# Score maps worked in pairs, and the sparse heads' normalising given to Pool

## The chip, the cores and the metric

The kernel runs on one core of one Trainium2 chip. A core has five engines that matter here: TensorE (PE, with its weight loads as PEld), VectorE (DVE), ScalarE (ACT), GpSimd (Pool, POOL in the rows) and SyncE (SP, which issues the transfers). The metric is the device time of one execution in microseconds (us). The time of the kernel before is a median of 760.54 us over 3 runs (760.04 to 768.84).

## The reference, cut to what matters

The program is a decoder trunk of two layers on 256 tokens of width 1024, in float32. Each layer is an attention part and a SwiGLU part, both with RMSNorm before, and a shift, a scale and a gate that come from a conditioning vector `c` (`ada_w`, six 1024-wide products a layer).

```python
h = rms_norm(x, attn_norm[i]) * (1.0 + sc_a) + sh_a
y = sparse_mixer(h, ...)  if i % 2 == 0 else  diff_mixer(h, ...)
x = x + g_a * y
h = rms_norm(x, ffn_norm[i]) * (1.0 + sc_f) + sh_f
x = x + g_f * swiglu(h, w_gate, w_up, w_down)
...
p = masked_softmax(q @ k.T * scale, causal)      # one map: 256 queries x 256 keys, 64 deep
o_nsa = g0 * o_c + g1 * (p_s @ v_s) + g2 * (p_w @ v_w)    # layer 0, 8 NSA heads, two full maps each
o_moba = p @ v                                   # layer 0, 8 MoBA heads, one map each
a = p[:, :, 0] - lam * p[:, :, 1];  o = a @ v    # layer 1, 8 differential heads, two maps each
```

With 256 tokens every block that the sparse heads could choose is taken, so their maps are plain causal ones. That makes 16 NSA maps, 8 MoBA maps and 16 differential maps: 40 in all. The 24 maps of layer 0 are divided by their row sums (for NSA also multiplied by a gate) before they meet the values; in layer 1 the division comes after the product.

## The kernel before, in words

A weight product is made from two-part numbers: `split` (L181 to L184) writes a high part with ACT (L182) and the rest with DVE (L183), and three products are added. Nearly every matmul goes through the helper `mm`, so L110 stands for all of them; they are told apart by the names of their tiles.

One softmax map is `softmax_map` (L799 to L813). Its causal 256x256 matrix lies in one PSUM bank as two parts: the first 128 queries against 128 keys (128 columns) and the other 128 queries against 256 keys (256 columns). PE makes both (four instructions, since a float32 matmul passes twice); for each part DVE masks, scales and finds the row extreme (L808), and ACT takes the exponential with its row sum (L810). `normalise` (L816) then multiplies by the factor: part 0 on ACT (L819), part 1 on DVE (L821). `transpose_map` (L824) turns the three 128x128 blocks on PE (L827) into another bank, and ACT copies them to SBUF (`pT`, L829). `av` (L832) multiplies with the values.

Queries and keys of a head take 64 of the 128 rows of PE, and its output 64 of the 128 columns: the even head of a pair stands on rows and columns 0 to 63, the odd one on 64 to 127. In `nsa_heads` (L1061) a pair `pr` runs over its two heads, a head over its two branches (`kTn`, `nkv` are the keys and values), and after both branches come `av` twice and a product for the compressed branch (`pcT` by `vblk`). `moba_heads` (L1100, keys and queries `kTm`, `qTm`, values `vm`) has one map for a head. `diff_heads` (L1134) makes two maps for a head and combines them; it has no `normalise`.

The order on each engine is set by a scheduler that simulates the program with its own costs; the Python generators hand it the work, and a `yield` is where `weave` (L40) may go over to another generator, by the shares written beside each. In layer 0 the heads are woven with `moba_proj` and `ada` at first, and then with `ada_pe` (L310): 16 steps, each a 512 KB transfer and a product on four groups of 32 columns of PE (`raw`, `cs` in the rows), that fill PE between the maps. After them comes the output projection with `sp_w_out`. The buffers: four `s` tiles (one a map), three `pT` tiles, five `raw` tiles; banks for scores `SC`, for transposes `TR` and for outputs `OT`.

Of the kernel before, what the change touches and what calls it, by code (L numbers as in the profile page):

```python
# [13 lines left out]
AF = mybir.ActivationFunctionType  # L14
ALU = mybir.AluOpType
AX = mybir.AxisListType

P = 128
S = 256
# [39 lines left out]
def tile_trunk(ctx: ExitStack, tc: tile.TileContext, x, c, positions, ada_w, ada_b, attn_norm, ffn_norm,  # L59
# [36 lines left out]
    def tmp(shape, tag, bufs, dt=F32):  # L96
        return sp.tile(shape, dt, name=nm(tag), tag=tag, bufs=bufs)
# [10 lines left out]
    def mm(o, lhsT, rhs, start, stop):  # L108

        ins = T.matmul(o, lhsT=lhsT, rhs=rhs, start=start, stop=stop).ins  # L110
        key = o.tensor.name
        if start and key in closed:
            tc.add_manual_dep(ins, closed[key], mybir.DependencyInfo(mybir.DependencyClass.NoSync,
                                                                    mybir.DependencyReason.DATA))
        if stop:
            closed[key] = ins.name
        if chain:
            if chain[0]:
                tc.add_manual_dep(ins, chain[0], mybir.DependencyInfo(mybir.DependencyClass.NoSync,
                                                                     mybir.DependencyReason.DATA))  # L120
            chain[0] = ins.name
        return ins
# [673 lines left out]
        return fcol[:, n:n + 1]  # L796


    def softmax_map(qh, kh, nr):  # L799

        b = bank(*SC)
        mm(b[:, 0:P], lhsT=qh[:, 0:P], rhs=kh[:, 0:P], start=True, stop=True)
        mm(b[:, P:P + S], lhsT=qh[:, P:S], rhs=kh, start=True, stop=True)
        s = tmp([P, 384], "s", 4)
        mx = tmp([P, 2], "mx", 6)
        sm = tmp([P, 2], "sm", 6)
        for t, (o, n) in enumerate(((0, P), (P, S))):
            V.tensor_tensor_reduce(out=s[:, o:o + n], in0=b[:, o:o + n], in1=maskc[:, S - n:S], scale=nr(t),  # L808
                                   scalar=3e38, op0=ALU.add, op1=ALU.min, accum_out=mx[:, t:t + 1])
            A.activation(out=s[:, o:o + n], in_=s[:, o:o + n], func=AF.Exp, scale=-1.0, bias=mx[:, t:t + 1],  # L810
                         accum_out=sm[:, t:t + 1])
        return s, sm

    SEG = ((0, P), (P, S))

    def normalise(s, sm):  # L816
        for t, (o, n) in enumerate(SEG):
            if t == 0:
                A.activation(out=s[:, o:o + n], in_=s[:, o:o + n], func=AF.Copy, scale=sm[:, t:t + 1])  # L819
            else:  # L820
                V.tensor_scalar(out=s[:, o:o + n], in0=s[:, o:o + n], scalar1=sm[:, t:t + 1], scalar2=None,  # L821
                                op0=ALU.mult)

    def transpose_map(s):  # L824
# [12 lines left out]

    def nsa_first(hts):
# [222 lines left out]
    def nsa_heads(oh, ol):  # L1061
        qT, nrs, kT, vv, gts, vblk, pcT = (box[k] for k in ("qT", "nrs", "kT", "vv", "gts", "vblk", "pcT"))
        for pr in range(4):
            g = pr // 2
            ob = None
            for half in range(2):
                h = pr * 2 + half
                rows = slice(half * 64, (half + 1) * 64)
                pTs = []
                for br in range(2):  # L1070
                    s, sm = softmax_map(qT[rows, pr, :], kT[rows, br, g, :], lambda t: nrs[:, t, h:h + 1])
                    V.reciprocal(out=sm, in_=sm)
                    V.tensor_tensor(out=sm, in0=sm, in1=gts[:, :, (1 + br) * 8 + h], op=ALU.mult)
                    normalise(s, sm)
                    pTs.append(transpose_map(s))
                    yield
                if ob is None:
                    ob = bank(*OT)
                o = ob[rows, 0:S]
                for br in range(2):  # L1080
                    av(o, lambda kc: vv[kc][:, 1 + br, g, :], pTs[br], br == 0, False)
                mm(o, lhsT=vblk[:, h, :], rhs=pcT, start=False, stop=True)
            anc.append(split(ob[:, 0:S], oh[:, pr, :], ol[:, pr, :])[::-1])
            yield

# [14 lines left out]
    def moba_heads(oh, ol):  # L1100
        qT, kT, v, nrs = (box2[k] for k in ("qT", "kT", "v", "nrs"))
        for pr in range(4):
            ob = None
            for half in range(2):
                h = pr * 2 + half
                rows = slice(half * 64, (half + 1) * 64)
                s, sm = softmax_map(qT[rows, pr, :], kT[rows, pr, :], lambda t: nrs[:, t, h:h + 1])
                V.reciprocal(out=sm, in_=sm)
                normalise(s, sm)
                pT = transpose_map(s)  # L1110
                if ob is None:
                    ob = bank(*OT)
                av(ob[rows, 0:S], lambda kc: v[kc][:, h * 64:(h + 1) * 64], pT, True, True)
                yield
            anc.append(split(ob[:, 0:S], oh[:, pr, :], ol[:, pr, :])[::-1])
            yield

# [16 lines left out]
    def diff_heads(part, st, oh, ol):  # L1134
# [15 lines left out]
        for pr in range(2):  # L1150
            od = tmp([P, 512], "od", 2).rearrange("p (h t d) -> p h t d", h=2, t=NT)
            ss = tmp([P, 4], "dss", 3)
            for h2 in range(2):
                hh = pr * 2 + h2
                ps = []
                for cmp_ in range(2):
                    rows = slice(cmp_ * 64, (cmp_ + 1) * 64)
                    ps.append(softmax_map(qT[rows, hh, :], kT[rows, hh, :],
                                          lambda t: nrs[:, t, hh * 2 + cmp_:hh * 2 + cmp_ + 1]))
                    yield  # L1160

                (s0, m0), (s1, m1) = ps
                V.reciprocal(out=m1, in_=m1)
# [32 lines left out]
    def late(*gens):  # L1196
        for g in gens:
            yield from g
# [71 lines left out]
```

## Time and profile before

| what | value |
|---|---|
| median of 3 runs | 760.54 us (760.04 to 768.84) |
| the profiled execution | 761.66 us, its span 760.0 us |
| mean granted TensorE clock | 0.973 |
| NSA and MoBA maps of layer 0 | about 82 to 202 us of the span |
| differential maps, part 0 with the projection of part 1 | about 470 to 530 us |
| PE, DVE, ACT, POOL busy over the span | 720.1, 499.3, 397.6, 49.3 us |

The profile is of one execution, and its own time is 1.1 us above the median. A busy share is a mean over the span; the rows further down are read from one stretch each, as time and length of a group of instructions.

### The profile page before, as it was taken

How to read it: one execution, taken by the hardware profiler on the slowest of the kernel's cores; microseconds unless marked ns; L12 is line 12 of the kernel's file. 1: busy time of each engine (PE TensorE's matmuls, PEld its weight loads, DVE VectorE, ACT ScalarE, POOL GpSimd, SP SyncE). 2: the span in 40 equal slices, each digit the busy share in tenths (PEclk: the TensorE clock that was granted, in tenths of full speed). 3: DMA queues.
4: the chain of work that ended last, by engine and by line, in shares of the span. 5: the costliest groups of instructions: out<-in, count | busy, mean ns of one | idle time of the engine just before them, and what ended most of it. 6: DMA issues, size and time to landing. Idle time of an engine off the chain costs nothing.

```text
span 760.0 us, 11877 instructions
## 1 busy us (share of the span) xinstructions
PE 720.1 (95%) x4414; PEld 586.9 (77%) x4414; DVE 499.3 (66%) x1032; ACT 397.6 (52%) x755; POOL 49.3 (6%) x131
## 2 busy tenths in 40 slices
PE   5889999999989999999999799979899999999997
PEld 1468567555679989999898578767679999999985
DVE  3558567654588788877776685787587584544532
ACT  3465635666666555345363566866466344434430
POOL 5004102000000000000000023230000000000000
PEclk9999899999999999999999999997889999999999
DMA  9965188126847999999995366152145886566501
GB/s 320 379 234 192 38 305 280 45 106 218 279 147 239 340 324 324 346 318 329 314 321 191 111 209 206 63 190 81 47 135 190 269 293 202 168 195 191 173 25 55
DMA packets 90625, 159.47 MB, mean 210 GB/s; under 512 B 6199, under 2 KB 56508, under 8 KB 90568
## 3 DMA queue, kind: packets, MB, share of 16 engines
q1 hardware_dynamic: 90088, 158.72, 62.1%
q8 instruction: 34, 0.56, 0.3%
q14 instruction: 23, 0.19, 0.1%
q0 software_dynamic: 480, 0.01, 0.0%
HBM read 157.66 MB, written 1.05 MB: 209 GB/s over the span
## 4 chain that ended last, share of the span: by engine, by line
PE 86%; ACT 4%; DVE 4%; DMA 3%; issue 2%; POOL 1%; SPq 0%; ACTq 0%; DVEq 0%
PE bank L110 82%; PE bank L827 2%; ACT s L810 1%; DMA vm<-in_ada_w_dram 1%; DMA tok<-in_ada_w_dram 1%; DVE lo L183 1%; ACT hi L182 1%; DMA raw<-in_sp_w_in_dram 1%; PE bank L632 1%; ACT bigT L182 1%; PE bank L393 1%; DVE w2k L402 0%; DVE bigT L183 0%; DVE s L1167 0%; DVE xs L428 0%
## 5 line engine op out<-in xcount | busy, mean ns | idle before, releaser
L183 DVE TENSOR_TENSOR lo<-raw,hi 128x1024 fp32r<-128x1024 f32 x144 | 172.3, 1208 | 88.5 <-ACT hi L182 87.9
L182 ACT ACTIVATE hi<-raw 128x1024 fp32r<-128x1024 f32 x144 | 149.2, 1047 | 132.7 <-PE bank L110 72.2
L110 PE MATMUL bank<-hi,bigT 128*128 128x512 f32 (+2 forms) x640 | 195.2, 382 | 15.0 <-ACT bigT L182 13.5
L110 PEld LDWEIGHTS bank<-hi,bigT 128*128 128x128 f32 x640 | 119.7, 198 | 41.8 <-ACT bigT L182 16.0
L110 PE MATMUL bank<-bigT,hi 128*128 128x256 f32 x768 | 140.0, 283 | 0.0
L110 PEld LDWEIGHTS bank<-bigT,hi 128*128 128x128 f32 x768 | 120.3, 191 | 1.7 <-issue 0.9
L110 PE MATMUL bank<-lo,bigT 128*128 128x512 f32 (+2 forms) x320 | 119.5, 374 | 0.0
L110 PE MATMUL bank<-bigT,lo 128*128 128x256 f32 x384 | 108.6, 283 | 0.0
L271 DVE SCALAR_TENSOR_TENSOR ada_acc<-araw,cs,ada_acc 128x1024 f32<-128x1024 f32 x60 | 76.8, 1280 | 30.3 <-DMA araw<-in_ada_w_dram 29.9
L110 PEld LDWEIGHTS bank<-bigT,lo 128*128 128x128 f32 x384 | 73.6, 192 | 0.0
L110 PEld LDWEIGHTS bank<-lo,bigT 128*128 128x128 f32 x320 | 63.2, 198 | 10.3 <-issue 1.4
L808 DVE CUSTOM_DVE_ANT_0 s<-bank,maskc,nrs 128x128 f32<-128x128 f32 x80 | 29.8, 414 | 31.4 <-PE bank L827 21.4
L810 ACT ACTIVATE s<-s,mx 128x128 f32<-128x128 f32 x80 | 35.6, 448 | 8.1 <-DVE mx L808 8.1
L152 POOL TENSOR_SCALAR rs_w<-ss 128x16 f32<-128x16 f32 x7 | 4.8, 684 | 430.7 <-DVE ss L610 388.7
L183 DVE TENSOR_TENSOR nkv<-raw,nkv 128x1024 fp32r<-128x1024 f32 x16 | 19.6, 1222 | 12.9 <-ACT nkv L182 12.9
L110 PE MATMUL bank<-hi,kTm 128*128 128x512 f32 x80 | 27.6, 402 | 0.0
L110 PE MATMUL bank<-hi,vm 128*128 128x512 f32 x80 | 27.5, 400 | 0.0
L182 ACT ACTIVATE nkv<-raw 128x1024 fp32r<-128x1024 f32 x16 | 16.9, 1055 | 20.1 <-PE bank L110 9.8
L183 DVE TENSOR_TENSOR tok<-raw,tok 128x1024 fp32r<-128x1024 f32 x18 | 22.0, 1221 | 5.7 <-ACT tok L182 5.5
L110 PE MATMUL bank<-bigT,nkv 128*128 128x256 f32 x192 | 25.7, 281 | 0.0
L427 DVE TENSOR_TENSOR xn<-bank,mod 128x512 f32<-128x512 f32 x16 | 11.0, 690 | 20.9 <-PE bank L110 20.9
L110 PE MATMUL bank<-bigT,tok 128*128 128x256 f32 x192 | 24.7, 277 | 0.0
(322 smaller groups left out, 1174.8 us busy)
## 6 DMA issues: line engine op xcount, KB each, us to landing
araw<-in_ada_w_dram SPq DMA_DIRECT2D x66, 512.0 KB, 5.0
raw<-in_ffn_w_gate_dram SPq DMA_DIRECT2D x44, 512.0 KB, 5.5
raw<-in_ffn_w_up_dram SPq DMA_DIRECT2D x44, 512.0 KB, 5.2
raw<-in_ffn_w_down_dram SPq DMA_DIRECT2D x44, 512.0 KB, 4.7
raw<-in_diff_w_in_dram SPq DMA_DIRECT2D x24, 512.0 KB, 5.1
raw<-in_sp_w_in_dram SPq DMA_DIRECT2D x20, 512.0 KB, 6.2
raw<-in_ada_w_dram SPq DMA_DIRECT2D x17, 512.0 KB, 4.8
raw<-in_nsa_cmp_w_dram SPq DMA_DIRECT2D x8, 512.0 KB, 4.7
```

Of the source, the lines that this page charges most:

```text
L110: ins = T.matmul(o, lhsT=lhsT, rhs=rhs, start=start, stop=stop).ins
L152: E.tensor_scalar(out=o, in0=i, scalar1=m, scalar2=c_, op0=ALU.mult, op1=ALU.add)
L182: i1 = A.activation(out=hi, in_=src, func=AF.Copy)
L183: i2 = V.tensor_tensor(out=lo, in0=src, in1=hi.bitcast(F32), op=ALU.subtract)
L271: ins = V.scalar_tensor_tensor(out=acc, in0=raw, scalar=cs[:, k:k + 1], in1=acc, op0=ALU.mult, op1=ALU.add)
L393: T.transpose(out=(b[k % 2] if type(b) is tuple else b)[:, k * P:(k + 1) * P], in_=xn[:, f * 512 + k * P:f * 512 + (k + 1) * P], identity= ...
L427: V.tensor_tensor(out=y, in0=bs[t][f], in1=g[:, fs], op=ALU.mult)
L632: T.transpose(out=b[:, k * P:(k + 1) * P], in_=src[:, k * P:(k + 1) * P], identity=ident)
L808: V.tensor_tensor_reduce(out=s[:, o:o + n], in0=b[:, o:o + n], in1=maskc[:, S - n:S], scale=nr(t), scalar=3e38, op0=ALU.add, op1=ALU.min, ...
L810: A.activation(out=s[:, o:o + n], in_=s[:, o:o + n], func=AF.Exp, scale=-1.0, bias=mx[:, t:t + 1], accum_out=sm[:, t:t + 1])
L827: T.transpose(out=b[:, k * P:(k + 1) * P], in_=s[:, k * P:(k + 1) * P], identity=ident)
```

## The change

Two heads' maps (for a differential head its two maps) are worked together. `softmax_maps` makes the first part of both scores, then the second part of both, and goes part by part through DVE and ACT. `av` takes the outputs, values and `pT` tiles of both heads and alternates between them. Pool multiplies both parts of a layer 0 map by the factors, in place of ACT and DVE. In `nsa_heads` the loop over branches is now inside the pair, a pair of maps ends with one `yield`, and `av` stands behind it. The `pT` tiles are four, the row extremes have a tile for each part, `first` takes 6 yields of the NSA heads into the first weave instead of 10, and the differential heads' share is 12 instead of 16.

```diff
-    def softmax_map(qh, kh, nr):
+    def softmax_maps(qks, nrs):
+        bs = [bank(*SC) for _ in qks]
+        for n in range(2):
+            for b, (qh, kh) in zip(bs, qks):
+                if n == 0:
+                    mm(b[:, 0:P], lhsT=qh[:, 0:P], rhs=kh[:, 0:P], start=True, stop=True)
+                else:
+                    mm(b[:, P:P + S], lhsT=qh[:, P:S], rhs=kh, start=True, stop=True)
+        res = [(tmp([P, 384], "s", 4), tmp([P, 2], "sm", 6)) for _ in qks]
         for t, (o, n) in enumerate(((0, P), (P, S))):
+            for b, nr, (s, sm) in zip(bs, nrs, res):
+                mx = tmp([P, 2], "mx", 6)
...
     def normalise(s, sm):
         for t, (o, n) in enumerate(SEG):
-            if t == 0:
-                A.activation(out=s[:, o:o + n], in_=s[:, o:o + n], func=AF.Copy, scale=sm[:, t:t + 1])
-            else:
-                V.tensor_scalar(out=s[:, o:o + n], in0=s[:, o:o + n], scalar1=sm[:, t:t + 1], scalar2=None,
-                                op0=ALU.mult)
+            G.tensor_scalar(out=s[:, o:o + n], in0=s[:, o:o + n], scalar1=sm[:, t:t + 1], scalar2=None, op0=ALU.mult)
...
-        pT = tmp([P, 384], "pT", 3)
+        pT = tmp([P, 384], "pT", 4)
...
-    def av(o, v, pT, first, last):
-        mm(o, lhsT=v(0), rhs=pT[:, 0:S], start=first, stop=False)
-        mm(o[:, P:S], lhsT=v(1), rhs=pT[:, S:S + P], start=False, stop=last)
+    def av(os, vs, pTs, first, last):
+        for o, v, pT in zip(os, vs, pTs):
+            mm(o, lhsT=v(0), rhs=pT[:, 0:S], start=first, stop=False)
+        for o, v, pT in zip(os, vs, pTs):
+            mm(o[:, P:S], lhsT=v(1), rhs=pT[:, S:S + P], start=False, stop=last)
...
+            for br in range(2):
+                res = softmax_maps([(qT[e * 64:(e + 1) * 64, pr, :], kT[e * 64:(e + 1) * 64, br, g, :])
+                                    for e in range(2)],
+                                   [lambda t, h=pr * 2 + e: nrs[:, t, h:h + 1] for e in range(2)])
                 pTs = []
+                for e, (s, sm) in enumerate(res):
                     V.reciprocal(out=sm, in_=sm)
...
                     normalise(s, sm)
                     pTs.append(transpose_map(s))
+                yield
+                av(os, [lambda kc: vv[kc][:, 1 + br, g, :]] * 2, pTs, br == 0, False)
+            for e, o in enumerate(os):
+                mm(o, lhsT=vblk[:, pr * 2 + e, :], rhs=pcT, start=False, stop=True)
...
-    weave((late(np_, first(nh, 10)), 22), (moba_proj(hts), 20), (ada(0, 2, pin=True), 9))
+    weave((late(np_, first(nh, 6)), 22), (moba_proj(hts), 20), (ada(0, 2, pin=True), 9))
...
-    weave((diff_heads(0, st, *oa), 16), (diff_proj(hts, 1, st), 18))
+    weave((diff_heads(0, st, *oa), 12), (diff_proj(hts, 1, st), 18))
```

The scheduler orders the engines anew. On PE in the heads of layer 0, before: `ident,s` are transposes of a map, `raw,cs` passes of `ada_pe`, `kTm,qTm` scores, `pT,nkv` the product with the values (256 columns, then 128), `pcT,vblk` the compressed branch.

```order
L827 MATMUL bank_71<-ident,s_1668 128x128 x3
L110 MATMUL bank_70<-raw_1704,cs 1x256 x4
L110 MATMUL bank_68<-kTm_787,qTm_786 128x128
L110 MATMUL bank_68<-kTm_787,qTm_786 128x256
L110 MATMUL bank_73<-pT_1645,nkv_110 64x256
L110 MATMUL bank_73<-pT_1645,nkv_111 64x128
L110 MATMUL bank_73<-pcT_1140,vblk_843 64x256
L827 MATMUL bank_72<-ident,s_1687 128x128 x3
L110 MATMUL bank_69<-kTm_787,qTm_786 128x128
L110 MATMUL bank_69<-kTm_787,qTm_786 128x256
```

And the same place in the changed kernel:

```order
L110 MATMUL bank_73<-pT_1639,nkv_110 64x256
L828 MATMUL bank_71<-ident,s_1668 128x128
L110 MATMUL bank_70<-raw_1888,cs 1x256 x4
L828 MATMUL bank_71<-ident,s_1668 128x128 x2
L110 MATMUL bank_73<-pT_1648,nkv_110 64x256
L110 MATMUL bank_73<-pT_1639,nkv_111 64x128
L110 MATMUL bank_73<-pT_1648,nkv_111 64x128
L110 MATMUL bank_73<-pcT_1140,vblk_843 64x256 x2
L828 MATMUL bank_72<-ident,s_1670 128x128
L110 MATMUL bank_68<-kTm_787,qTm_786 128x128
L110 MATMUL bank_68<-kTm_787,qTm_786 128x256
L828 MATMUL bank_72<-ident,s_1670 128x128 x2
```

The two heads' `pT,nkv` products stand together except for the first one's 256 columns, the two `pcT,vblk` products stand together, and some maps' three transposes are cut into one and two with other work between. Scores are still ordered one map after the other in this piece.

On POOL in layer 0, of the changed kernel: `rs_a`, `rs_y` are steps of the inverse root that scales the MoBA keys, twelve small operations in a row before; L823 is the new multiplication.

```order
L155 TENSOR_TENSOR rs_a_931<-rs_a_931,rs_w_929 128x16
L823 TENSOR_SCALAR s_1161<-s_1161,sm_1162 128x128
L823 TENSOR_SCALAR s_1161<-s_1161,sm_1162 128x256
L823 TENSOR_SCALAR s_1238<-s_1238,sm_1239 128x128
L823 TENSOR_SCALAR s_1238<-s_1238,sm_1239 128x256
L823 TENSOR_SCALAR s_1240<-s_1240,sm_1241 128x128
L823 TENSOR_SCALAR s_1240<-s_1240,sm_1241 128x256
L161 TENSOR_SCALAR rs_a_931<-rs_a_931 128x16
```

Six of the new operations stand between two steps of that chain, and two more a step ahead of them.

On PE in layer 1, at the end of the projection of part 1, before: the last two of 24 weight products (`hi`, `lo` by `bigT`), and then the transposes of keys and queries (L632, `tok`), of a head's output (L1145) and of a map.

```order
L110 MATMUL bank_67<-lo_5057,bigT_2134 128x512
L110 MATMUL bank_67<-hi_5056,bigT_2135 128x512
L632 MATMUL bank_73<-ident,tok_4688 128x128 x4
L632 MATMUL bank_74<-ident,tok_4893 128x128 x4
L1145 MATMUL bank_70<-ident,od_4586 128x128 x2
L632 MATMUL bank_73<-ident,tok_4893 128x128 x4
L827 MATMUL bank_73<-ident,s_4947 128x128 x3
L110 MATMUL bank_68<-kTm_4564,qTm_4563 128x128
```

In the changed kernel the 24 weight products begin behind those transposes (their first two are shown):

```order
L632 MATMUL bank_74<-ident,tok_4725 128x128 x4
L632 MATMUL bank_73<-ident,tok_4725 128x128 x4
L828 MATMUL bank_74<-ident,s_4796 128x128 x3
L632 MATMUL bank_73<-ident,tok_4929 128x128 x4
L110 MATMUL bank_70<-vm_4270,pT_4838 128x128 x3
L632 MATMUL bank_74<-ident,tok_4929 128x128 x4
L828 MATMUL bank_73<-ident,s_4979 128x128 x3
L110 MATMUL bank_69<-kTm_4588,qTm_4587 128x128
L1145 MATMUL bank_70<-ident,od_4610 128x128 x2
L110 MATMUL bank_67<-hi_4996,bigT_2156 128x512
L110 MATMUL bank_67<-lo_4997,bigT_2156 128x512
```

What moved: the transposes that needed the keys and queries now have the weight products behind them instead of ahead of them.

## Rows read from the trace of the kernel before

**Rows 1.** Page: busy us (share of the span) and instructions; chain by engine.

```profile
PE 720.1 (95%) x4414; PEld 586.9 (77%) x4414; DVE 499.3 (66%) x1032; ACT 397.6 (52%) x755; POOL 49.3 (6%) x131
...
PE 86%; ACT 4%; DVE 4%; DMA 3%; issue 2%; POOL 1%; SPq 0%; ACTq 0%; DVEq 0%
```

**Rows 2.** Windows of 60 us: PE, PEld, DVE, ACT, POOL busy, clock, DMA share, GB/s.

```profile
140.00:200.00 60.00, 58.73 (x378) 31.54 (x376) 30.02 (x133) 40.98 (x129) 0.00 (x0) 1.00 0.42 145
```

**Rows 3.** Timeline, PE, 140 to 200 us: start, length, line, tiles, PE rows*columns, shape.

```profile
152.50 0.55 PE L827 MATMUL bank<-ident,s 128*128 128x128 f32 x3
152.98 0.92 PE L110 MATMUL bank<-kTn,qT 64*128 64x128 f32 x4
153.83 0.86 PE L110 MATMUL bank<-pT,nkv 128*64 128x256 f32 x4
154.62 0.87 PE L827 MATMUL bank<-ident,s 128*128 128x128 f32 x6
155.43 0.92 PE L110 MATMUL bank<-kTn,qT 64*128 64x128 f32 x4
156.28 0.86 PE L110 MATMUL bank<-pT,nkv 128*64 128x256 f32 x4
156.98 0.59 PE L110 MATMUL bank<-pcT,vblk 128*64 128x256 f32 x2
157.50 0.92 PE L110 MATMUL bank<-kTn,qT 64*128 64x128 f32 x4
...
174.96 0.59 PE L110 MATMUL bank<-raw,cs 128*1 128x256 f32 x2
...
177.29 0.61 PE L110 MATMUL bank<-raw,cs 128*1 128x256 f32 x8
...
180.39 0.93 PE L110 MATMUL bank<-kTm,qTm 64*128 64x128 f32 x8
```

**Rows 4.** Groups by line and shape, ACT, then DVE, 140 to 200 us.

```profile
L810 ACT ACTIVATE s<-s,mx 128x256 f32<-128x256 f32 x18 | 9.0, 501 | 0.0
L819 ACT ACTIVATE s<-s,sm 128x128 f32<-128x128 f32 x18 | 6.9, 394 | 1.0 <-DVE sm L1073 0.8 <-DVE sm L1108 0.2
...
L183 DVE TENSOR_TENSOR lo<-raw,hi 128x1024 fp32r<-128x1024 f32 x4 | 4.8, 1224 | 3.8 <-ACT hi L182 3.8
```

**Rows 5.** Groups by line and shape, POOL, whole span.

```profile
L766 POOL TENSOR_SCALAR_AFFINE_SELECT maskc<-maskc 128x256 f32<-128x256 f32 x1 | 0.5, 467 | 0.0
...
L130 POOL TENSOR_SCALAR_AFFINE_SELECT ident<-ones 128x128 f32<-128x128 f32 x1 | 0.3, 284 | 0.0
```

**Rows 6.** Timelines, POOL and DVE, around 63 and 89 us.

```profile
63.49 1.16 POOL L152 TENSOR_SCALAR rs_y<-rs_w 128x16 int32<-128x16 int32 x1
...
63.37 1.23 DVE L183 TENSOR_TENSOR lo<-raw,hi 128x1024 fp32r<-128x1024 f32 x1
...
88.85 0.20 POOL L152 TENSOR_SCALAR rs_y<-rs_w 128x16 int32<-128x16 int32 x1
```

**Rows 7.** Timeline, PE, around 510 us; in brackets the idle time before.

```profile
509.36 0.66 PE L632 MATMUL bank<-ident,tok 128*128 128x128 f32 x4 [2.44 <-ACT kTm L633]
511.55 0.90 PE L827 MATMUL bank<-ident,s 128*128 128x128 f32 x3 [1.53 <-ACT qTm L633]
```

**Rows 8.** Windows of 5 us around there, columns as in rows 2.

```profile
510.00:515.00 5.00, 3.46 (x16) 2.54 (x15) 3.68 (x9) 2.41 (x7) 0.00 (x0) 0.50 0.83 261
515.00:520.00 5.00, 5.00 (x21) 3.61 (x21) 4.66 (x24) 4.07 (x19) 0.00 (x0) 0.50 0.63 209
520.00:525.00 5.00, 5.00 (x24) 3.70 (x24) 3.59 (x18) 3.44 (x16) 0.00 (x0) 0.63 0.00 0
```

**Rows 9.** Chains of waits around 95 us and 500 us: start, length, what.

```profile
94.30 5.79 DMA raw<-in_sp_w_in_dram
...
500.34 5.48 PE bank L110 x24
...
514.57 2.27 ACT s L810 x10
```

More of the change, by code (lines that the diff above doesn't have):

```diff
@@ L796, in fc @@
         return fcol[:, n:n + 1]
-    def softmax_map(qh, kh, nr):
[L801 to L806, printed above, removed]
-        for t, (o, n) in enumerate(((0, P), (P, S))):
[L808 to L812, printed above, removed]
+    def softmax_maps(qks, nrs):
[7 more added lines that the diff above has]
+        res = [(tmp([P, 384], "s", 4), tmp([P, 2], "sm", 6)) for _ in qks]
+        for t, (o, n) in enumerate(((0, P), (P, S))):
+            for b, nr, (s, sm) in zip(bs, nrs, res):
+                mx = tmp([P, 2], "mx", 6)
+                V.tensor_tensor_reduce(out=s[:, o:o + n], in0=b[:, o:o + n], in1=maskc[:, S - n:S], scale=nr(t),
+                                       scalar=3e38, op0=ALU.add, op1=ALU.min, accum_out=mx[:, t:t + 1])
+                A.activation(out=s[:, o:o + n], in_=s[:, o:o + n], func=AF.Exp, scale=-1.0, bias=mx[:, t:t + 1],
+                             accum_out=sm[:, t:t + 1])
+        return res
     SEG = ((0, P), (P, S))
@@ L1064, in nsa_heads @@
             g = pr // 2
[L1065 to L1068, printed above, removed]
+            ob = bank(*OT)
+            os = [ob[e * 64:(e + 1) * 64, 0:S] for e in range(2)]
+            for br in range(2):
+                res = softmax_maps([(qT[e * 64:(e + 1) * 64, pr, :], kT[e * 64:(e + 1) * 64, br, g, :])
+                                    for e in range(2)],
+                                   [lambda t, h=pr * 2 + e: nrs[:, t, h:h + 1] for e in range(2)])
                 pTs = []
-                for br in range(2):
-                    s, sm = softmax_map(qT[rows, pr, :], kT[rows, br, g, :], lambda t: nrs[:, t, h:h + 1])
+                for e, (s, sm) in enumerate(res):
                     V.reciprocal(out=sm, in_=sm)
-                    V.tensor_tensor(out=sm, in0=sm, in1=gts[:, :, (1 + br) * 8 + h], op=ALU.mult)
+                    V.tensor_tensor(out=sm, in0=sm, in1=gts[:, :, (1 + br) * 8 + pr * 2 + e], op=ALU.mult)
                     normalise(s, sm)
                     pTs.append(transpose_map(s))
[L1076 to L1082, printed above, removed]
+                yield
+                av(os, [lambda kc: vv[kc][:, 1 + br, g, :]] * 2, pTs, br == 0, False)
+            for e, o in enumerate(os):
+                mm(o, lhsT=vblk[:, pr * 2 + e, :], rhs=pcT, start=False, stop=True)
             anc.append(split(ob[:, 0:S], oh[:, pr, :], ol[:, pr, :])[::-1])
@@ L1102, in moba_heads @@
         for pr in range(4):
[L1103 to L1107, printed above, removed]
+            res = softmax_maps([(qT[e * 64:(e + 1) * 64, pr, :], kT[e * 64:(e + 1) * 64, pr, :]) for e in range(2)],
+                               [lambda t, h=pr * 2 + e: nrs[:, t, h:h + 1] for e in range(2)])
+            pTs = []
+            for s, sm in res:
                 V.reciprocal(out=sm, in_=sm)
                 normalise(s, sm)
[L1110 to L1114, printed above, removed]
+                pTs.append(transpose_map(s))
+            yield
+            ob = bank(*OT)
+            av([ob[e * 64:(e + 1) * 64, 0:S] for e in range(2)],
+               [lambda kc, h=pr * 2 + e: v[kc][:, h * 64:(h + 1) * 64] for e in range(2)], pTs, True, True)
             anc.append(split(ob[:, 0:S], oh[:, pr, :], ol[:, pr, :])[::-1])
@@ L1154, in diff_heads @@
                 hh = pr * 2 + h2
[L1155 to L1160, printed above, removed]
+                ps = softmax_maps([(qT[e * 64:(e + 1) * 64, hh, :], kT[e * 64:(e + 1) * 64, hh, :]) for e in range(2)],
+                                  [lambda t, h=hh * 2 + e: nrs[:, t, h:h + 1] for e in range(2)])
+                yield
                 (s0, m0), (s1, m1) = ps
```

## The prediction, as it was made
> **What bounds the kernel now.** I read the page first, for the engine that sets the pace: PE is busy 95% of the span and 86% of the chain that ended last runs over it, while POOL has 6% [rows 1]. Then the stretch that the change touches most, layer 0's heads: from 140 to 200 us PE is busy 58.73 of 60 us at the full clock, ACT 40.98, DVE 30.02, POOL not at all [rows 2]. So taking work from ACT and DVE buys next to nothing by itself; what counts is how long PE's own instructions take there, and the timeline of PE prices them one by one [rows 3]. Last, layer 1's heads, where PE is not full: it stands idle 2.44 and 1.53 us for ACT's copies of keys and queries [rows 7], and its clock is at the lower of its two levels, 1.2 instead of 2.4 GHz, for 5 + 5 + (1 - 0.63) x 2 x 5 = 13.7 us [rows 8].
>
> **Prices of PE's pieces**, from one start to the next in [rows 3]: three transposes of a map 152.98 - 152.50 = 0.48; six 155.43 - 154.62 = 0.81, so three more cost 0.33 and a group of its own 0.15; scores of one map 153.83 - 152.98 = 0.85; its product with the values (AV) 154.62 - 153.83 = 0.79; the compressed branch (PC) 157.50 - 156.98 = 0.52. Two maps' scores that stand side by side, eight instructions on both halves of PE's rows, last 0.93 against 0.92 for four: the second map is free. The same holds for groups of columns, shown by the passes of `ada_pe`: eight on four groups last 0.61, two on one group 0.59.
>
> **The change on PE, layer 0.** The work is the same; what is saved is counted in the new order.
> - Scores: of 24 maps seven pairs stand side by side and ten maps alone, so 17 times 0.85 are paid; before there were about 21. Saved: 4 x 0.85 = 3.4.
> - AV: twelve pairs. In one all four steps are adjacent, which saves one map's 0.79. In eleven the first head's 256 columns stand alone (0.15 + 2/3 of 0.64 = 0.58) and the other three steps follow together (0.43 + 0.21 + 0.15 = 0.79): 1.37 against 1.58 saves 0.21. Together 11 x 0.21 + 0.79 = 3.1.
> - PC: eight become four pairs: 4 x 0.52 = 2.1.
> - Transposes: twelve maps' three transposes are cut in two, others are joined; groups go from 23 to 32: 9 x 0.15 = 1.35 lost. This row is a price that PE pays at each change of the tile shape. The Trainium skill, "TensorEngine Tiling (Array Packing)", Key Properties, says that a change of tiling mode drains the engine, which speaks against cutting these groups; it gives no figure, and its other property, that tiles work independently, is what the eight-instruction row shows.
>
> Sum 3.4 + 3.1 + 2.1 - 1.35 = 7.3, taken as 7. Bounds: if nothing on different columns overlaps, as it does for `ada_pe` but is not shown for AV, AV and PC give nothing and 3.4 - 1.35 = 2 is left. If every pair overlapped fully, scores would save 9 x 0.85, AV 12 x 0.79, PC 2.1: 19. I stay near the count, since it is made of rows at each term.
>
> **POOL's new work.** 24 maps times two operations. No row shows a 128x256 multiply there; the nearest are its 128x128 and 128x256 selects, 0.284 and 0.467 [rows 5], which I take: 0.75 a map, 1.5 a pair, about 1.8 with gaps. From below the 0.20 of a small one; from above 1.16, what the same small one took while DVE ran `lo<-raw,hi`, 1.23 long, from 63.37 [rows 6]. PE needs per pair of NSA maps 2 x (0.85 + 0.48 + 0.79) + 0.52 = 4.76 before and, less 7.3 / 12, about 4.15 after. So POOL at 1.8 hides behind PE. Its factors come later than now: ACT and DVE did the two parts at once in 0.394 [rows 4], and the second map of a pair now waits 1.5, some 1.1 longer; four `s` tiles let the other pair's 4.15 of PE work stand in between, so I cost that at nothing. If that cover were gone it would be 12 x 1.1 = 13. ACT and DVE lose one operation each per map, off the path, costed at nothing. On POOL's queue the eight multiplications within the chain of the MoBA keys make it end some 3 us later (four maps at 0.75); the projection's next weights land 5.79 after 94.30 [rows 9], and PE has other work until then, so again nothing; uncovered it would be 3. The transfers keep their order; `ada_pe` ends earlier among the heads and the output weights move in between, off the path. The fourth `pT` and the separate extremes take a wait away at most, nothing.
>
> **Layer 1.** The scores of a head's two maps stood side by side already, so pairing gains nothing there. What moves is the 24 weight products, 5.48 us [rows 9], from ahead of the transposes to behind them, with ACT's copies ahead of four splits. At best both idle times go, 3.97, and of the half clock about 2, since the chain after it runs over ACT's exponentials, 2.27 [rows 9], and not over PE alone: 6. At worst the products then wait for their own splits and nothing is won: 0. I take 1.5, about one of the two idle times, for the products still have to be done before the heads of part 1 and the exponentials set the pace behind them.
>
> **Sum.** -7 - 1.5 = -8.5 on the profiled execution's 761.66 gives 753.2; that execution stands 1.1 above the median of the runs, so **752** is the predicted time. A measurement of this kernel can tell about 2%, 15 us, from no change.
>
> **Rivals.**
> - *Layer 1 opens up.* Idle times and lower clock both go: 4.5 more, 747; with the pairs of layer 0 at somewhat better than the count, 743. For: ACT's copies, which released both waits [rows 7], now stand ahead of the splits. Against: the exponentials behind. Chance 0.14.
> - *POOL becomes the pace* (slower). Each multiplication shares its time with a DVE operation of two SBUF inputs and takes 1.2 as in [rows 6]; four and gaps make 5.1 a pair, more than PE's 4.76 before: 12 x 0.35 = +4, and PE's holes may bring its clock to the lower level, at most another 6.8 for a stretch as long as the 13.7 in [rows 8]: 765 to 771. It decides from (4.15 - 0.3) / 4 = 0.96 an operation; beyond +2% it is at 4.76 + 15.2 / 12 = 6.0 a pair, 1.4 an operation. Against: from 140 to 200 us there are only four such DVE operations of 1.22 [rows 4]; the first pairs and the last MoBA pairs meet more. Chance 0.12, a third of it beyond 2%. The Trainium skill, "SBUF — State Buffer", Who interferes with whom, has this as a rule: a DVE instruction with two SBUF inputs holds the shared read port against a GpSimd one that reads SBUF, and the later one waits in full. The two lengths of the small operation agree with it, 1.16 beside such an instruction and 0.20 without.
> - *Pairing doesn't do what it says.* The instructions stand close but the first of each pair waits for the second head's `pT` or bank, and the saved time comes back as waits (most of the 7): 757 to 762. For: PE takes its instructions in order, and both heads' exponentials now come before one AV. Chance 0.19.
> - *Full overlap in layer 0*, all 19: 740. Against: the counted order. Chance 0.03.
>
> My forecast, 747 to 757, has the remaining 0.52. The range 743 to 766 leaves out the last case and the part of the second beyond it. Faster by over 2%, below 745.3: 0.03 and half of the first, 0.10. Slower, above 775.7: 0.04. Within 2%: 0.86.
>
> **What would show it.** Right: in the heads of layer 0 PE stays busy, the count of AV and PC groups falls, adjacent AV steps of two heads last about 0.8, the new multiplications last near 0.3 and 0.45, and the output projection starts some 7 us earlier. Layer 1: the idle time before L632 shrinks. Wrong: multiplications of 1 us and more, PE waiting for POOL ahead of transposes, a clock below 1.00 between 90 and 200 us, or AV pairs that last 1.6 in spite of standing together.

## The result, and the profile after

The changed kernel takes 766.72 us (median of 20 runs, 762.45 to 774.45), the kernel before 761.13 us beside it (median of 20). The ratio is **1.0072, interval 1.0049 to 1.0094**: slower by some 5.5 us, where I had forecast 752 us in a range of 743 to 766. The profiled execution of the changed kernel took 762.45 us, 4.3 below its median, and its span is 760.7 us: it lies with the fastest executions, so one loss below had to be read from the experiments' profiles too.

The page, busy times and chain, against [rows 1]:

```profile
PE 712.7 (94%) x4414; PEld 577.5 (76%) x4414; DVE 492.3 (65%) x1008; ACT 392.2 (52%) x731; POOL 87.4 (11%) x179
...
PE 81%; ACT 5%; DVE 4%; issue 4%; DMA 4%; POOL 1%; SPq 1%; POOLq 0%; ACTq 0%; DVEq 0%
```

PE is busy 7.4 us less than before, and the span is no shorter: what PE saves comes back as idle time. In the heads of layer 0 this is seen in a window of 60 us as in [rows 2], then in the slowest ten, then in what follows (length; PE, PEld, DVE, ACT, POOL busy; clock):

```profile
140.00:200.00 60.00, 58.12 (x373) 31.08 (x372) 29.27 (x117) 38.22 (x113) 29.90 (x36) 0.91 0.57 191
142.00:152.00 10.00, 9.18 (x42) 5.93 (x42) 4.66 (x19) 5.12 (x19) 3.85 (x4) 0.52 0.00 1
160.00:208.00 48.00, 48.00 (x322) 25.41 (x315) 23.73 (x79) 29.74 (x80) 21.76 (x26) 1.00 0.81 271
```

From 142 to 152 us the clock is 0.52, nearly all at the lower level; from 160 us on PE has no gap. The timeline of PE just ahead of the slow ten and within it (start, length, idle before in brackets):

```profile
139.74 0.44 PE L1056 MATMUL bank<-ident,scc 128*128 128x128 f32 x2 [2.87 <-DVE scc L1052]
140.65 0.55 PE L828 MATMUL bank<-ident,s 128*128 128x128 f32 x3 [0.47 <-ACT pcT L1058]
141.78 1.11 PE L632 MATMUL bank<-ident,tok 128*128 128x128 f32 x4 [0.58 <-ACT pT L830]
146.67 1.11 PE L110 MATMUL bank<-pT,nkv 128*64 128x256 f32 x4 [0.82 <-ACT pT L830]
```

The same transposes before, without a wait, and in the kernel of experiment 11 below, which has the pairs but not POOL's multiplications:

```profile
138.67 0.44 PE L1053 MATMUL bank<-ident,scc 128*128 128x128 f32 x2
```

```profile
136.55 0.44 PE L1060 MATMUL bank<-ident,scc 128*128 128x128 f32 x2 [2.35 <-DVE scc L1056]
```

PE waits 2.87 us for the compressed branch's scores (`scc`), which go through DVE in a chain; before there was no wait ahead of them. The wait comes with the pairs, whoever multiplies. The likely reason, which no run isolates, is that PE is done sooner with the pairs and has no other work at the end of the projections. The granted clock falls right behind the first two of these gaps.

The new multiplications on POOL, grouped by shape, then a piece of POOL's timeline in which they stand in the chain of the MoBA keys' inverse root, and DVE's instruction beside the last of them:

```profile
L823 POOL TENSOR_SCALAR s<-s,sm 128x256 f32<-128x256 f32 x24 | 23.8, 993 | 0.0
L823 POOL TENSOR_SCALAR s<-s,sm 128x128 f32<-128x128 f32 x24 | 17.2, 718 | 36.3 <-DVE sm L1076 10.1 <-ACT s L815 9.9 <-DVE sm L1108 8.7
...
89.32 1.51 POOL L823 TENSOR_SCALAR s<-s,sm 128x128 f32<-128x128 f32 x2
90.80 0.21 POOL L155 TENSOR_TENSOR rs_a<-rs_a,rs_w 128x16 f32<-128x16 f32 x1
91.00 5.30 POOL L823 TENSOR_SCALAR s<-s,sm 128x128 f32<-128x128 f32 x6
96.39 0.26 POOL L161 TENSOR_SCALAR rs_a<-rs_a 128x16 f32<-128x16 f32 x1
...
93.61 1.23 DVE L183 TENSOR_TENSOR lo<-raw,hi 128x1024 fp32r<-128x1024 f32 x1 [3.22 <-ACT hi L182]
```

They take 0.72 and 0.99 us on the mean, 3.4 a pair, where I had taken 0.28 and 0.47 from [rows 5]. Eight of them hold the keys' chain up for 1.51 + 5.30 = 6.8 us; I had said 3. PE's matmuls do not wait for either: from 81 to 219 us the trace has no gap of 0.15 us or more on PE that ends with POOL's work or with the MoBA keys. Only its weight loads waited for POOL, eight times and 3.2 us in all.

In layer 1, ACT's timeline (squares L609, copies of keys and queries L633) and POOL's last step of the queries' inverse root (`nrs`); of the changed kernel first:

```profile
501.34 1.26 ACT L633 ACTIVATE kTm<-bank,fcol 128x512 f32<-128x512 f32 x2 [0.79 <-PE bank L632]
505.57 0.59 ACT L633 ACTIVATE qTm<-bank 128x512 f32<-128x512 f32 x1
507.51 1.08 ACT L609 ACTIVATE w2k<-bank 128x512 f32<-128x512 f32 x2
...
509.50 0.20 POOL L152 TENSOR_SCALAR rs_w<-ss 128x16 f32<-128x16 f32 x1 [15.01 <-DVE ss L610]
517.05 0.20 POOL L655 COPY nrs<-rs_y 128x16 f32<-128x16 f32 x1
...
505.73 0.94 PE L110 MATMUL bank<-vm,pT 128*128 128x128 f32 x6 [2.41 <-ACT pT L830]
...
518.37 1.32 PE L110 MATMUL bank<-kTm,qTm 64*128 64x128 f32 x8 [1.04 <-DVE mx L813]
```

and of the kernel before, the same work:

```profile
499.17 1.08 ACT L609 ACTIVATE w2k<-bank 128x512 f32<-128x512 f32 x2
500.90 0.71 ACT L633 ACTIVATE kTm<-bank,fcol 128x512 f32<-128x512 f32 x1
...
508.10 1.07 POOL L655 COPY nrs<-rs_y 128x16 f32<-128x16 f32 x1
```

The squares stood ahead of the copies and now stand behind three of the four copies, 8.3 us later, of which 1.1 is the later start of the stage. The inverse root, a chain of small POOL operations of some 7 us, ran beside the 24 weight products; now it begins at 509.50, about when they do, and ends 7 us later in its stage than before. No exponential of part 1 can start without it: the last row has PE waiting 1.04 us for `mx`, which DVE makes with `nrs`.

### The profile page after: what moved, and what is told of

The parts are those of the page before. It is cut to its first block, busy times and chain, and to the rows that moved or that the text cites. A ratio compares the mean times of both kernels' runs of the same rounds, so it can differ in the third digit from the quotient of the medians.

```text
span 760.7 us, 11923 instructions
## 1 busy us (share of the span) xinstructions
PE 712.7 (94%) x4414; PEld 577.5 (76%) x4414; DVE 492.3 (65%) x1008; ACT 392.2 (52%) x731; POOL 87.4 (11%) x179
## 4 chain that ended last, share of the span: by engine, by line
PE 81%; ACT 5%; DVE 4%; issue 4%; DMA 4%; POOL 1%; SPq 1%; POOLq 0%; ACTq 0%; DVEq 0%
PE bank L110 77%; DMA raw<-in_sp_w_in_dram 3%; PE bank L828 2%; DVE lo L183 2%; ACT hi L182 1%; DMA xs<-in_x_dram 1%; PE bank L393 1%; ACT bigT L182 1%; ACT s L815 1%; PE bank L632 1%; POOL rs_a L155 0%; DVE s L813 0%; ACT xn L380 0%; POOL rs_b L155 0%; ACT w2k L407 0%
## 5 line engine op out<-in xcount | busy, mean ns | idle before, releaser
L110 PE MATMUL bank<-hi,bigT 128*128 128x512 f32 (+2 forms) x640 | 190.7, 375 | 15.8 <-ACT bigT L182 13.9
L110 PEld LDWEIGHTS bank<-hi,bigT 128*128 128x128 f32 x640 | 117.3, 195 | 41.4 <-ACT bigT L182 17.0
L813 DVE CUSTOM_DVE_ANT_0 s<-bank,maskc,nrs 128x128 f32<-128x128 f32 (+1 forms) x80 | 29.9, 414 | 30.8 <-PE bank L828 20.3
L823 POOL TENSOR_SCALAR s<-s,sm 128x128 f32<-128x128 f32 (+1 forms) x48 | 40.3, 855 | 36.3 <-DVE sm L1076 10.1
L815 ACT ACTIVATE s<-s,mx 128x128 f32<-128x128 f32 (+1 forms) x80 | 35.7, 448 | 12.4 <-DVE mx L813 12.3
```

The costliest lines, as they stand in the source:

```text
L823: G.tensor_scalar(out=s[:, o:o + n], in0=s[:, o:o + n], scalar1=sm[:, t:t + 1], scalar2=None, op0=ALU.mult)
```

## The experiments

Ratios are to the kernel before, measured on the same chip. Theory A: POOL's price took the gain. B: the new order of the pairs did. C: layer 1 did.

**1. The factors back on ACT and DVE, pairs kept.**

```diff
-            G.tensor_scalar(out=s[:, o:o + n], in0=s[:, o:o + n], scalar1=sm[:, t:t + 1], ...)
+            if t == 0:
+                A.activation(out=s[:, o:o + n], in_=s[:, o:o + n], func=AF.Copy, scale=sm[:, t:t + 1])
+            else:
+                V.tensor_scalar(out=s[:, o:o + n], in0=s[:, o:o + n], scalar1=sm[:, t:t + 1], ...)
```

> The pairs stay, but the factors are multiplied as before: part 0 by ACT, part 1 by DVE. The changed kernel stands at 1.0072 of before. Theory A (POOL's two multiplications take 0.60 and 0.92 us instead of the 0.28 and 0.47 that I took, so a pair of maps waits some 3 us for them, and PE's saved 7.4 us go into waits and a lower clock): the waits go and the saving comes out, 0.990 to 0.999 of before. Theory B (the waits come from the new order of the pairs and of the projections around them, whoever multiplies): 1.003 to 1.010, as the changed kernel.

Measured: 755.29 us, 0.9894 (0.9852 to 0.9936). A, and by a little more than its range: without POOL the change gains. With POOL it loses, but that loss is layer 1's, as experiment 3 shows.

**2. POOL alone**, single maps: experiment 1's edit the other way, in the kernel before.

> The kernel before with one edit: POOL multiplies both parts of a layer 0 map; maps stay single. Theory A: a map's transposes come 1.5 us after its sums instead of 0.4, PE has no more slack than before, and nothing is saved on PE: slower, 1.003 to 1.012. Theory B: 0.998 to 1.002, POOL hides behind PE.

Measured: 764.19 us, 1.0038 (1.0001 to 1.0074), at the lower end of what A expected; the interval reaches into B's range too.

**3. Layer 1 as before**, in the changed kernel.

```diff
-                ps = softmax_maps([(... both maps ...)], [...])
-                yield
+                for e in range(2):
+                    ps += softmax_maps([(... map e ...)], [...])
+                    yield
...
-    weave((diff_heads(0, st, *oa), 12), (diff_proj(hts, 1, st), 18))
+    weave((diff_heads(0, st, *oa), 16), (diff_proj(hts, 1, st), 18))
```

> The changed kernel with layer 1 as before: a differential head's two maps one after the other with a yield each, share 16. Theory A: layer 1 has no part in it, 1.004 to 1.010 as the changed kernel. Theory C (layer 1's new order, where the inverse roots on POOL and the AV products now wait, costs the loss in most executions, though not in the profiled one): 0.997 to 1.002.

Measured: 760.17 us, 0.9996 (0.9964 to 1.0028). C: layer 1 costs 0.7% by itself, and with POOL the pairs of layer 0 neither gain nor lose. The profile of the changed kernel alone had not shown this.

**4. The product with the values for one head, then the other.**

```diff
         for o, v, pT in zip(os, vs, pTs):
             mm(o, lhsT=v(0), rhs=pT[:, 0:S], start=first, stop=False)
-        for o, v, pT in zip(os, vs, pTs):
             mm(o[:, P:S], lhsT=v(1), rhs=pT[:, S:S + P], start=False, stop=last)
```

> The changed kernel, but the product with the values is made for one head and then for the other, so their 128 column steps don't alternate. If two heads' AV on different columns run beside each other and the time counts at the end, some 2 to 5 us are lost: 1.009 to 1.014. If PE's saving goes into waits anyway (theory A or B): 1.005 to 1.009, as the changed kernel, with PE's busy time up by 2 to 3 us.

Measured: 765.38 us, 1.0027 (0.9995 to 1.0060), below both expectations. This does not isolate the alternation, for the scheduler ordered PE's other work anew: 17 runs of scores and 31 groups of transposes, against 18 and 34 in the changed kernel. Whether the alternation gains or loses time in the whole stays open.

**5. Experiments 1 and 3 together.**

> Pairs in layer 0 alone, factors multiplied by ACT and DVE, layer 1 as before. The two edits measured apart: factors back on ACT and DVE 0.9894 of before, layer 1 back alone 0.9996 against the changed kernel's 1.0072. Theory C (layer 1's new order costs some 0.7% by itself): they add, 0.979 to 0.986. Theory A alone (layer 1 counts nothing): 0.987 to 0.993.

Measured: 752.78 us, 0.9893 (0.9845 to 0.9942). The two don't add here: experiment 1 alone had as much. Layer 1 was long in experiment 1's profile (123.70 us, as counted below) and short in this one's (113.81). But the first is of the slowest of six executions (758.67 us) and the second of the fastest of six (747.03), and the ratios don't tell the two kernels apart. Why layer 1's loss does not show beside ACT's and DVE's pairs stays open.

**6. Layer 1's part of the change alone**, in the kernel before.

> The kernel before with layer 1's part of the change alone: its two maps in a pair and the share 12. Theory C: 1.004 to 1.011 of before, with PE's waits in the stretch of its heads. My forecast had 1.5 us less, 0.998. If layer 1 counts nothing: 0.997 to 1.003.

Measured: 767.32 us, 1.0086 (1.0054 to 1.0118). C, clearly: the whole net loss of the change is there without any of its work in layer 0.

**7 and 8. POOL multiplies one part only**, in the changed kernel: the first part, with DVE on the second; then the second, with ACT on the first.

```diff
-            G.tensor_scalar(...)
+            if t == 0:      # experiment 8: t == 1, and ACT's copy otherwise
+                G.tensor_scalar(...)
+            else:
+                V.tensor_scalar(...)
```

> The changed kernel, but POOL multiplies only the first part of a map (0.60 us), DVE the second. Theory A by length: POOL's 1.2 us a pair are as short as I had taken for both parts; the order holds 15 runs of scores and 22 groups of transposes, near the 14 and 21 of the kernel with ACT and DVE (18 and 34 in the changed one): 0.989 to 0.997. If any work on POOL in this chain costs as much (its start, its queue): 1.002 to 1.008.

> The changed kernel, but POOL multiplies only the second part of a map (0.92 us), ACT the first. Theory A by length: POOL takes 1.84 us a pair, between the first-part kernel's 1.2 and the changed kernel's 3.0: 0.990 to 1.000, at or above the first-part kernel. If any work on POOL costs as much: 1.002 to 1.008.

Measured: 763.64 us, 1.0022 (0.9992 to 1.0052) and 760.31 us, 0.9978 (0.9944 to 1.0012). The first lies where any work on POOL was to cost as much, the second where length was to decide. Both lie between experiment 1 and the changed kernel, so giving POOL both parts costs more than giving it one; that the smaller part costs no less than the larger is against a loss by length alone. In their profiles the heads of layer 0, in the window that is explained below, take 133.2 and 132.7 us, between 127.0 in experiment 11 and 137.9 in the changed kernel.

**9. The share of layer 1's heads, 11 for 12**, in the changed kernel: one number.

```diff
-    weave((diff_heads(0, st, *oa), 12), (diff_proj(hts, 1, st), 18))
+    weave((diff_heads(0, st, *oa), 11), (diff_proj(hts, 1, st), 18))
```

It puts ACT's squares ahead of the copies of the keys again; the maps stay in pairs. The share sets the order of the whole stage, so other work moves too.

> The changed kernel with one number changed: the share of layer 1's heads is 11 instead of 12. In the changed kernel ACT's squares of part 1's queries (L609) stand behind its copies of the keys, so the inverse root on POOL ends 9 us later than before; with 11 the squares stand ahead of the copies again, and the maps are still in pairs. Theory D (the squares' place in ACT's queue costs layer 1's 5 us): 0.996 to 1.003 of before. If it is the pairing itself: 1.004 to 1.010.

Measured: 760.01 us, 1.0002 (0.9974 to 1.0029). ACT's and POOL's timelines of this run:

```profile
501.93 1.08 ACT L609 ACTIVATE w2k<-bank 128x512 f32<-128x512 f32 x2
503.65 0.71 ACT L633 ACTIVATE kTm<-bank,fcol 128x512 f32<-128x512 f32 x1
...
510.69 1.07 POOL L655 COPY nrs<-rs_y 128x16 f32<-128x16 f32 x1
```

**10. The kernel before with 12 for 16**, all maps single: the squares go behind the copies.

> The kernel before with one number changed: the share of layer 1's heads is 12 instead of 16; all maps stay single. ACT's squares of part 1's queries then stand behind its copies of the keys, as in the changed kernel. Theory D: slower by about as much as with the pairs, 1.004 to 1.011. If it is the pairing: 0.997 to 1.003.

Measured: 768.17 us, 1.0088 (1.0049 to 1.0126). One number, no pair, and the loss is there; with the pairs and 11 it is gone. Its rows:

```profile
497.96 1.26 ACT L633 ACTIVATE kTm<-bank,fcol 128x512 f32<-128x512 f32 x2 [0.92 <-PE bank L632]
503.60 1.08 ACT L609 ACTIVATE w2k<-bank 128x512 f32<-128x512 f32 x2
...
513.87 0.20 POOL L655 COPY nrs<-rs_y 128x16 f32<-128x16 f32 x1
```

Counted from one matmul of part 0's projection (470.05 us before, 471.15, 472.80 and 468.32 in the others), `nrs` is done after 39.1 us before, 46.1 in the changed kernel, 39.0 with 11, and 45.7 here.

**11. Pairs, ACT and DVE, share 11**: what the experiments point to.

> Pairs in both layers, factors by ACT and DVE, share 11. Theories A and D together: the layer 0 gain without layer 1's loss, 0.980 to 0.989 of before. If layer 1's pairing itself costs: 0.988 to 0.994.

Measured: **750.27 us, 0.9878 (0.9827 to 0.9929)**, the fastest, though experiments 1 and 5 can't be told from it, and the interval leaves both expectations open.

**12. The same, with the first four NSA heads as single maps**, so that no pair stands beside the projection's end.

```diff
+            if pr < 2:
+                ... for each head e and branch br: softmax_maps of one map, normalise, transpose_map, yield; then av
+            else:
                 for br in range(2):
                     res = softmax_maps(...)
...
-    weave((late(np_, first(nh, 6)), 22), ...)
+    weave((late(np_, first(nh, 10)), 22), ...)
```

> As the kernel with pairs, ACT and DVE and share 11, but the first four NSA heads, which are woven with the projections, are worked as single maps as before; pairs only from the fifth head on. Theory E (pairs beside the projection's end leave PE without work, 2.4 to 2.9 us ahead of the compressed branch's transposes, and bring the clock down after): that wait shrinks to under 1 us, the clock stays at its upper level from 130 to 152 us, and the time is the same or lower, 0.980 to 0.988 of before. If the pairs save more there than they lose: 0.986 to 0.994, above the kernel with all pairs.

Measured: 757.49 us, 0.9945 (0.9916 to 0.9974). Theory E's forecast fails in each part: the wait shrinks from 2.35 us in experiment 11 to 1.29, not to under 1, the clock still drops, and the time is longer.

```profile
138.83 0.44 PE L1060 MATMUL bank<-ident,scc 128*128 128x128 f32 x2 [1.29 <-DVE scc L1056]
...
140.00:150.00 10.00, 8.73 (x35) 4.79 (x35) 3.28 (x17) 6.40 (x20) 0.00 (x0) 0.67 0.00 0
80.47:214.74 134.27, 130.56 (x726) 80.20 (x726) 82.44 (x260) 78.62 (x213) 8.74 (x25) 0.95 0.56 192
```

The second row is a window of ten us: its clock is 0.67. The third is the window over layer 0's heads that is explained below: PE is idle for 134.27 - 130.56 = 3.7 us, 3.2 less than in experiment 11, but it is busy 10.4 us longer, 5 of it work at the full clock. The single maps cost more on PE than the shorter waits gave back; what a stretch without the wait would do was not tested.

**13 and 14. The engine crossed with PE's order.** With POOL the scheduler spreads the pairs on PE (18 runs of scores, 34 groups of transposes: the loose order) and with ACT and DVE it doesn't (14 and 21: the tight order). A table of the 805 matmuls of layer 0, in the order of the other kernel, is laid on PE by ordering edges, once on POOL's kernel of experiment 9, once on experiment 11's. The matmuls have the same numbers in both programs, so the table holds for either. The scheduler still orders the other engines around it: in experiment 14 some 8% of DVE's and ACT's instructions of this stretch stand elsewhere than in 11.

```diff
+PE_ORDER = (...)                      # 805 numbers
...
+    for x, y in zip(PE_ORDER, PE_ORDER[1:]):
+        tc.add_manual_dep(T.by[f"I-{y}"], f"I-{x}", mybir.DependencyInfo(mybir.DependencyClass.NoSync, ...))
```

> POOL multiplies, share 11, but PE's 805 matmuls of layer 0 stand word for word in the order of the kernel where ACT and DVE multiply (14 runs of scores and 21 groups of transposes instead of 18 and 34). POOL with its own order was 1.0002 of before, ACT and DVE 0.9878. Theory F (what was lost is PE's order, which the scheduler spread because POOL's operations are long): 0.985 to 0.993. Theory G (what was lost is POOL's length itself: PE then waits ahead of the transposes, some 1.1 us at each of twelve pairs): 0.997 to 1.012.

> The other way round: ACT and DVE multiply, share 11, but PE's 805 matmuls of layer 0 stand in the order of the kernel where POOL multiplies. Theory F: the order alone costs, 0.996 to 1.003 of before, as with POOL. Theory G: without POOL's length the wait is gone, 0.985 to 0.993.

Measured: 760.52 us, 0.9990 (0.9964 to 1.0016), and 759.85 us, 0.9997 (0.9966 to 1.0029). Neither F nor G: each alone costs all that both cost together.

| | PE's order of POOL's kernel | PE's order of ACT's and DVE's |
|---|---|---|
| POOL multiplies | 1.0002 | 0.9990 |
| ACT and DVE multiply | 0.9997 | 0.9878 |

The profiles show where the time goes. These are windows over the heads of layer 0, from the same matmul ahead of the heads to the same one in the output projection: the kernel before, the changed one, experiment 11, experiment 9, 13, 14 (each from its own trace).

```profile
81.11:217.78 136.67, 134.31 (x725) 84.09 (x725) 81.56 (x260) 78.29 (x213) 8.80 (x25) 0.98 0.55 189
```

```profile
81.13:219.04 137.91, 130.85 (x726) 79.22 (x726) 75.37 (x236) 71.82 (x189) 46.74 (x73) 0.95 0.55 187
```

```profile
81.35:208.40 127.05, 120.14 (x726) 75.50 (x726) 81.36 (x260) 77.02 (x213) 6.51 (x25) 0.99 0.59 203
```

```profile
80.10:218.21 138.11, 129.03 (x726) 78.13 (x726) 75.42 (x236) 71.51 (x189) 46.54 (x73) 0.96 0.55 187
```

```profile
81.41:221.18 139.77, 125.92 (x726) 78.91 (x726) 75.95 (x236) 71.04 (x189) 45.56 (x73) 0.94 0.54 185
```

```profile
79.90:217.99 138.09, 130.06 (x726) 79.17 (x726) 81.52 (x260) 78.21 (x213) 6.63 (x25) 0.95 0.55 187
```

Idle is the length less PE's busy time; what the clock took is busy time by (1 - clock); the rest is PE's work at its full clock, in us. The clock is printed with two digits, so the last two columns are good to some 0.7 us, and each row is one execution:

| kernel | length | idle | clock | rest |
|---|---|---|---|---|
| before | 136.7 | 2.4 | 2.7 | 131.6 |
| changed | 137.9 | 7.1 | 6.5 | 124.3 |
| 9: POOL, own order | 138.1 | 9.1 | 5.2 | 123.8 |
| 14: ACT and DVE, POOL's order | 138.1 | 8.0 | 6.5 | 123.6 |
| 13: POOL, the other order | 139.8 | 13.9 | 7.6 | 118.4 |
| 11: ACT and DVE, own order | 127.0 | 6.9 | 1.2 | 118.9 |

The lengths repeat. The changed kernel and experiments 3 and 9 have the same order of instructions on every engine in this stretch, and took 137.9, 137.6 and 138.1 us; so have experiments 1, 5 and 11, and took 128.6, 126.7 and 127.0. The rest follows PE's order, 124 or 119, and the prices of the prediction give that: 4 runs of scores at 0.85 and 13 groups at 0.15 are 5.4. Idle time does not set the changed kernel apart from experiment 11, 7.1 against 6.9. With the tight order POOL pays in waits; the largest, in experiment 13's timeline of PE, is for the MoBA keys (line numbers are that file's):

```profile
104.90 1.11 PE L107 MATMUL bank<-ident,tok 128*128 128x128 f32 x4 [5.71 <-DVE tok L676]
```

DVE comes to these keys late because POOL's inverse root, with the eight multiplications in it, ended at 99.08 there, and a split of the next weights stood ahead of the last steps on DVE. That is a cover that I had costed at nothing; it held in the changed kernel's loose order and failed in the tight one. In experiment 14 the rest is 4.7 longer and the clock takes 5.3 more than in 11; why the clock falls there for longer, with idle time only 1.1 longer, one profile doesn't tell. Part of it may be the execution: experiments 1 and 11 run the same order in layer 0, and after the same wait of 2.35 us their clocks differ (windows of ten us, experiment 1 and then 11):

```profile
137.00:147.00 10.00, 7.34 (x37) 4.71 (x38) 3.43 (x18) 5.29 (x18) 0.00 (x0) 0.66 0.00 1
```

```profile
138.00:148.00 10.00, 7.90 (x48) 5.20 (x47) 5.39 (x23) 6.46 (x22) 0.00 (x0) 0.83 0.00 0
```

## Why the prediction was wrong

**PE's saving: right.** I took 7.3 us; PE's own work fell from 131.6 to 124.3, by 7.3, which is good to about 1 us. The exact fit is in part luck: the trace has 18 runs of scores and 34 groups of transposes where I had counted 17 and 32, which by the same prices leaves 6.1. For experiment 11's order they give 7 x 0.85 + 3.1 + 2.1 + 2 x 0.15 = 11.5, against 12.7 in the table. The prices hold in the timeline of PE after the change, piece by piece as in [rows 3]:

```profile
162.25 0.65 PE L110 MATMUL bank<-pT,nkv 128*64 128x256 f32 x2
162.82 0.33 PE L828 MATMUL bank<-ident,s 128*128 128x128 f32 x1
163.08 0.60 PE L110 MATMUL bank<-raw,cs 128*1 128x256 f32 x6
163.62 0.44 PE L828 MATMUL bank<-ident,s 128*128 128x128 f32 x2
163.99 0.86 PE L110 MATMUL bank<-pT,nkv 128*64 128x256 f32 x6
164.78 0.33 PE L828 MATMUL bank<-ident,s 128*128 128x128 f32 x1
```

The first head's 256 columns take 162.82 - 162.25 = 0.57 (0.58 taken), the pair's other three steps 164.78 - 163.99 = 0.79 (0.79 taken), a map's transposes cut in two 0.26 + 0.37 = 0.63 (0.48 + 0.15).

**Layer 0, taking PE's saving for time saved: wrong, and it cost all of it.** The sum has -7 for layer 0, and the delays that the prediction names beside it are each costed at nothing. Idle time rose by 4.7 us and the clock took 3.8 more, 8.5 together, so the stretch is 1.2 longer instead of 7 shorter. The two covers that I had named (the other pair's work for the later factors, the next weights at the MoBA keys) both held in the changed kernel. What the sum has no term for are waits that come with the pairs in other chains, 2.87 us for `scc` and 1.04 and 0.65 us at the start of the heads, and the clock at its lower level for nearly all of the ten us after the wait for `scc`. Experiment 11 has the same idle time, 6.9, without POOL's multiplications, and still gains: its tight order saves PE 5 us more and its clock takes 1.2 instead of 6.5. So the waits come with the pairs (theory B) and the loose order with POOL (theory A); for the clock's share there are only single executions. The rival that "the saved time comes back as waits" had the outcome of layer 0, and its 757 to 762 fits experiment 3, 760.17; its mechanism, waits for the second head's `pT`, is the smaller part (0.58 and 0.82 us). It had 0.19.

**POOL's price: less than half of what it was.** 0.72 and 0.99 us against 0.28 and 0.47: I took the selects on the same tile shapes for a multiply by a factor per row. The undisturbed ones took 0.60 and 0.92, above both rows and inside my bound of 1.16. "POOL becomes the pace" did not happen, as it should not by its own point: the mean of the two is 0.86, under 0.96, and from 160 to 208 us PE is never idle. POOL counted in another way: with it the scheduler gave PE the loose order, which costs 5 us. My count of 7.3 was of that order, so the 5 us are in it; I did not see that with ACT and DVE it would have been about 12.

**Layer 1, "I take 1.5": wrong sign, and the bound was wrong.** I bounded it by 6 and by 0, "at worst nothing is won". It cost 0.7 to 0.9%, 5 to 7 us (experiments 3, 6, 9, 10), all of the change's net loss. From the matmul at 470.05 to the one at 590.00, past the output projection, the nine profiles with the squares ahead of the copies took 113.8 to 120.0 us, mean 116.5, and the seven with the squares behind 119.6 to 124.2, mean 122.4: 5.9 more. In the changed kernel's own profile it was 119.63 against 119.95 before, because the clock there was 0.96 against 0.89; a comparison of the two profiles by themselves would have acquitted layer 1 (before, then changed):

```profile
470.05:590.00 119.95, 110.26 (x598) 89.86 (x596) 91.38 (x270) 78.93 (x205) 10.45 (x25) 0.89 0.39 124
```

```profile
471.15:590.78 119.63, 106.83 (x598) 85.59 (x597) 91.28 (x270) 79.29 (x204) 10.53 (x25) 0.96 0.38 124
```

What failed is the tracing of one queue. I saw that ACT's copies came ahead of the splits, and credited PE's idle time; I did not ask which of ACT's instructions the copies had passed. They had passed the squares, with a chain of 7 us behind them on POOL. PE's waits for the copies [rows 7] do go in the changed kernel, but in their place it waits 2.41 us for `pT` at 505.73 and then for `mx`; experiment 9 has the waits for the copies again, 1.50 and 1.08 us, and no loss. That the share carries the loss is shown by experiments 9 and 10. That it acts through the squares is read from the rows: they and `nrs` are late in all seven, but the share moves PE's work as well, and PE's idle time explains 3.0 of the 5.9 us on the mean (12.8 against 9.9).

**The sum.** +1.2 in layer 0 and +5 to 6 in layer 1 against -7 and -1.5. The median moved by 5.6, where I had forecast -8.5.

**The lock between DVE and POOL.** The rule of the Trainium skill, "SBUF — State Buffer", Who interferes with whom, that a DVE instruction with two SBUF inputs keeps a GpSimd one that reads SBUF waiting, agrees with the multiplication that took 1.35 us from 93.96 beside DVE's `lo<-raw,hi`, 1.23 from 93.61, against 0.60 for its like. It was a minor part: means of 0.72 and 0.99 against 0.60 and 0.92.

## What to carry to other kernels

When an edit moves rows of an engine's queue, list what was passed, not only what moved up: the instruction that lost its place may feed the longer chain. An edit that shortens the bottleneck's work can lay bare waits of other chains that no row of before shows, so time saved on it is an upper bound until these have a term. A delay that one order of the bottleneck hides (the MoBA keys in the changed kernel) can cost 5.7 us in another (experiment 13). Where a scheduler orders the program, a number in a weave can cost more than the edit beside it, so cross the two (the engine with the old order, the old engine with the new order) before naming the cause.

## What the runs showed of the hardware

POOL's multiply of 128 rows by a factor per row took 0.60 us for 128 columns and 0.92 for 256, about 2.5 ns a column; its selects on the same shapes 0.28 and 0.47, about 1.4. With the first head's long step done ahead, the other three of two heads' four steps, on two column groups of PE, took 0.79 us, as long as one head's two. The granted clock fell to its lower level close behind a gap of PE of 1.29 us in experiment 12 and of 2.35 to 2.87 us in the changed kernel and experiments 1 and 11. How long it stayed there was not the same for the same order of instructions: the two windows of experiments 1 and 11 above come to 2 x 0.34 x 10 = 6.8 us and 2 x 0.17 x 10 = 3.4 us.
